# The first block of a weight-stationary unit takes its 256-column matmul first

## The chip, the cores and the metric

The kernel runs on one core of one Trainium2 chip. The metric is the device time of one execution in microseconds. Before the change the median of three runs is 2078.01 us (2077.91 to 2078.08).

## The reference

A two-layer trunk on 256 tokens of width 2048, all in float32. Layer 0 is gated linear attention (4 heads) with an MLP behind it, then one shared K/V projection, then layer 1 with stick-breaking attention (16 query heads on 4 K/V heads) and a second MLP. Every weight is used once. Cut to what matters here:

```python
def sq_relu_mlp(x, w_up, w_down):                  # w_up 2048 x 8192, w_down 8192 x 2048
    return jnp.square(jax.nn.relu(x @ w_up)) @ w_down

h = h + gla_mixer(rms_norm(h, norm1_g[0]), ...)    # q, k, v, r, gate and output projections
h = h + sq_relu_mlp(rms_norm(h, norm2_g[0]), mlp_w_up[0], mlp_w_down[0])
k_sh, v_sh = shared_kv(h, kv_norm_g, kv_w)
h = h + stick_breaking_mixer(rms_norm(h, norm1_g[1]), sb_w_q[0], k_sh, v_sh, sb_w_out[0])
h = h + sq_relu_mlp(rms_norm(h, norm2_g[1]), mlp_w_up[1], mlp_w_down[1])
return rms_norm(h, final_g)
```

## The kernel before, in words

All products keep nearly full float32 precision by splitting: a value is a high part, rounded to the `fp32r` format that TensorE takes, plus a low part, the rest. A product of two split values is three products: high by high, high by low, low by high.

Weights stream from HBM in pieces of 1 MB (128 partitions by 2048 columns, tile `raw`). Each piece is handled as two halves of 1024 columns. For each half ScalarE makes the high part `wh` (L177) and VectorE the low part `wl` = raw - wh (L178). There are three buffers for `wh` and three for `wl`; `next_half()` keeps three halves ready, so that the split of a half starts when TensorE has finished the half three places earlier. `split_weights` shifts each half inside its buffer by a few columns so that all weights of one kind start at the same address modulo 128 columns.

Two kinds of projection use the halves.

- `chunk_n` (through `unit_n` and `half_n`, L232 to L234) keeps activations stationary and streams weights. Each of its matmuls has 512 columns, and three of them (low by high, high by high, high by low) follow each other into one PSUM bank. The second MLP product `dn`, `v`, `r`, `op` and `sv` are of this kind.
- `unit_t` keeps weights stationary and streams activations, so that its result comes out transposed. One unit makes 128 output features for 256 tokens. It goes over 16 blocks `kt` of 128 input features (eight in each half). Its activation tile `act[:, kt, :]` holds the 256 high columns and then the 256 low columns of the block. So a block is two matmuls: `high()` (L199) with `wh` against all 512 columns, and `low()` (L202) with `wl` against the 256 high columns alone. The bank's left half collects wl by high plus wh by high, its right half wh by low; `joined` adds the halves afterwards (ScalarE copy L217, VectorE add L218). Two PSUM banks (`psB`) take turns. The units are `qk` (16), `alow` (1), `up` (128: two MLPs with 4 quarters of 16 units), `sk` (4) and `sq` (16).

`start=True` on a matmul begins a bank's sums anew; all others add. The first block does `high()` and then `low()`, since the full-width matmul begins the sums of the whole bank. The other 15 blocks do `low()` and then `high()`.

An MLP quarter is 16 `up` units followed by four `dn` chunks. In the `qk` and `sq` stages small attention steps are pushed in between the halves (`pump`); their matmuls (`gate`, `cross`, `lev`, `z`, `tail`, `ao`) then stand between those of a unit. The order on each engine is else nearly that of the code; the builder moves a matmul ahead of another whose input is not ready yet at a few places (the first matmul of an MLP stands ahead of some transposes).

Of the kernel before, what the change touches and what calls it, by code (L numbers as in the profile page):

```python
# [16 lines left out]
P = 128  # L17
D = 2048
KT = D // P
T = 256  # L20
# [19 lines left out]
def yoco_kernel(ctx: ExitStack, tc: tile.TileContext, a: dict):  # L40
    nc = tc.nc
    V, S, PE = nc.vector, nc.scalar, nc.tensor
# [36 lines left out]
    def pump(n=1):  # L79
        for _ in range(n):  # L80
            while pending:
                try:
                    next(pending[0])
                    break
                except StopIteration:
                    pending.pop(0)
# [94 lines left out]
    def next_half():  # L181
        while len(ready) < 3:
            n = len(ready)
            prefetch()
            if len(ready) == n:
                break
        return ready.pop(0)


    def unit_t(act, name, steps=1):  # L190
        ps = psB.tile([P, 512], F32, tag="psB", name=name)
        for kt in range(KT):
            if kt % 8 == 0:
                wh, wl = next_half()
            o = (kt % 8) * P
            first, last = kt == 0, kt == KT - 1

            def high():
                PE.matmul(ps, wh[:, o:o + P], act[:, kt, :], start=first, stop=last)  # L199

            def low():
                PE.matmul(ps[:, 0:T], wl[:, o:o + P], act[:, kt, 0:T], start=False, stop=False)  # L202

            if first:
                high()
                low()
            else:
                low()
                high()
            if kt % 8 == 7:  # L210
                pump(steps)
        return ps
# [28 lines left out]
    def chunk_n(act, name):  # L241
        pss = banks(name)
        for kg in range(4):
            unit_n(pss, act, kg)
        return pss
# [278 lines left out]
    def queries_keys():  # L524
        qT = g512("qk", 4, "qT").rearrange("p (f t) -> p f t", f=2)
        kT = g512("qk", 4, "kT").rearrange("p (f t) -> p f t", f=2)
        for dst in (qT, kT):
            for f in range(2):
                joined(unit_t(xg, "qk"), dst[:, f])
        return qT, kT  # L530

    for hd in range(GLA_H):
        st = [half.tile([P, P], F32, tag=f"st{t}", name=f"st{t}", bufs=1) for t in range(NT)]
        sx = half.tile([P, P], F32, tag="sx", name="sx", bufs=1)
        if hd == 0:
            pv, pr = banks("v"), banks("r")
            for kg in range(4):
                unit_n(pv, xg, kg)
                unit_n(pr, xg, kg)
            qT, kT = queries_keys()  # L540
            drain()
            vv = values(pv)
            gs = gates(pr)
            araw = t256("araw")
            spread(rstd0, rbc0, 1.0)
            joined(unit_t(xg, "alow"), araw[0:16], rows=16)
            V.tensor_tensor(alow, araw[0:16], rbc0[0:16], op=ALU.mult)
            give(scores(hd, qT, kT, st, sx))
        else:
            qT, kT = queries_keys()  # L550
            give(scores(hd, qT, kT, st, sx))
            vv = values(chunk_n(xg, "v"))
            gs = gates(chunk_n(xg, "r"))
        give(outputs(hd, st, sx, vv, gs))
# [21 lines left out]
    def mlp(act, rstd2, ssq, after, last=None):  # L576
        for q in range(NQ):
            hT = act_tile("hT", actc if q % 2 else actp)
            for f in range(KT):
                ps = unit_t(act, "up")  # L580
                s = t256("s")
                joined(ps, s)
                y = t256("y")
                V.scalar_tensor_tensor(y, s, 0.0, s, op0=ALU.max, op1=ALU.mult)
                S.copy(hT[:, f, 0:T], y)
                V.tensor_tensor(hT[:, f, T:2 * T], y, hT[:, f, 0:T].bitcast(F32), op=ALU.subtract)
            for c in range(NCH):
                if q == NQ - 1 and c == NCH - 1 and last is not None:
                    last(hT)
                    return  # L590
                ps = chunk_n(hT, "dn")
                for t in range(NT):
                    hc = h[:, t, c * CH:(c + 1) * CH]
                    V.scalar_tensor_tensor(hc, ps[t], rstd2[:, t:t + 1], hc, op0=ALU.mult, op1=ALU.add)
                if q == NQ - 1:
                    squares(ssq, c)
                    after(c)
# [49 lines left out]
    ps = chunk_n(xkv, "sv")  # L647
# [95 lines left out]
    for n in range(KVH):  # L743
        qs = [t512(f"q{t}") for t in range(NT)]
        for g in range(GRP):
            ps = unit_t(xq, "sq", 1 + (len(pending) > 1 or g == GRP - 1))
# [130 lines left out]
```

## Time and profile before

| what | value |
|---|---|
| median of three runs | 2078.01 us |
| the profiled execution's own time | 2078.17 us |
| its span, first to last instruction | 2076.4 us |
| TensorE (PE) busy | 2060.9 us, 99%, 10544 matmuls |
| weight loads (PEld) busy | 1752.9 us, 84% |
| VectorE (DVE) busy | 1311.3 us, 63% |
| ScalarE (ACT) busy | 1038.3 us, 50% |
| DMA engines' mean busy share | 53.7% (queue 1) |
| granted TensorE clock, mean | 0.998 |

TensorE is busy for nearly the whole span, so the time is that of its stream of matmuls. Matmuls overlap in the trace: one is listed with 0.28 us (256 columns) or 0.39 us (512 columns), but the next one starts well before its end. What counts is the distance from the start of one matmul to the start of the next.

### The profile page before, as it was taken

The page shows a single profiled execution, that of the slowest core. Times are in us where ns is not written, and L with a number is a line of the kernel's source. Part 1 is how long each engine was busy: PE and PEld are TensorE (multiplying, and loading weights), DVE is VectorE, ACT ScalarE, POOL GpSimd, SP SyncE. Part 2 cuts the span into 40 slices and gives each one's busy share as a digit, 9 for nine tenths or more (in the row PEclk, how much of TensorE's full clock was granted, in tenths as well). Part 3 has the DMA queues.
Part 4 walks back from the last instruction along what each step waited for, and adds up shares of the span by engine and source line. Part 5 has one row for each costly group of instructions (what it writes and reads, how often), then busy time and mean ns, then how long its engine had stood idle before and what let it go on. Part 6 is the DMA issues. An engine that isn't in the chain of part 4 may idle for free.

```text
span 2076.4 us, 26656 instructions
## 1 busy us (share of the span) xinstructions
PE 2060.9 (99%) x10544; PEld 1752.9 (84%) x10544; DVE 1311.3 (63%) x1804; ACT 1038.3 (50%) x1447; POOL 0.4 (0%) x5
## 2 busy tenths in 40 slices
PE   8999999999999999999999999999999999999998
PEld 7888888888888888888888888888888888888886
DVE  5767776576556556556666687666556556655655
ACT  6645655554344435434555487645345434434543
POOL 0000000000000000000000000000000000000000
PEclk9999999999999999999999999999999999999999
DMA  8544444555555555555555644555555555555553
GB/s 317 183 163 145 160 164 164 183 183 197 189 197 188 200 185 198 189 201 184 201 184 183 208 157 142 183 183 192 193 195 191 197 188 196 190 200 186 198 189 141
DMA packets 55742, 388.40 MB, mean 187 GB/s; under 512 B 6449, under 2 KB 6961, under 8 KB 9153
## 3 DMA queue, kind: packets, MB, share of 16 engines
q1 hardware_dynamic: 55616, 386.70, 53.7%
q8 instruction: 83, 1.36, 0.3%
q14 instruction: 43, 0.34, 0.0%
HBM read 384.58 MB, written 2.10 MB: 186 GB/s over the span
## 4 chain that ended last, share of the span: by engine, by line
PE 99%; DVE 0%; ACT 0%; DMA 0%; issue 0%; DVEq 0%; SPq 0%
PE up L199 22%; PE up L202 11%; PE dn L234 11%; PE dn L233 11%; PE dn L232 11%; PE sq L199 3%; PE op L232 3%; PE op L234 3%; PE op L233 3%; PE qk L199 3%; PE v L232 1%; PE v L234 1%; PE v L233 1%; PE r L232 1%; PE sq L202 1%; PE r L234 1%
## 5 line engine op out<-in xcount | busy, mean ns | idle before, releaser
L178 DVE TENSOR_TENSOR wl<-raw,wh 128x1024 fp32r<-128x1024 f32 (+1 forms) x715 | 874.0, 1223 | 574.9 <-ACT wh L177 562.5
L177 ACT CAST wh<-raw 128x1024 fp32r<-128x1024 f32 (+1 forms) x715 | 750.8, 1051 | 706.1 <-PE dn L233 383.2
L199 PE MATMUL up<-xm,wh 128*128 128x512 f32 x2048 | 693.2, 390 | 0.0
L202 PE MATMUL up<-xm,wl 128*128 128x256 f32 x2048 | 546.3, 277 | 0.0
L199 PEld LDWEIGHTS up<-xm,wh 128*128 128x128 f32 x2048 | 375.4, 188 | 71.5
L202 PEld LDWEIGHTS up<-xm,wl 128*128 128x128 f32 x2048 | 384.4, 188 | 10.7
L234 PE MATMUL dn<-wl,hT 128*128 128x512 f32 x992 | 386.4, 389 | 0.0
L233 PE MATMUL dn<-wh,hT 128*128 128x512 f32 x992 | 386.3, 389 | 0.0
L232 PE MATMUL dn<-wh,hT 128*128 128x512 f32 x992 | 386.0, 389 | 0.0
L233 PEld LDWEIGHTS dn<-wh,hT 128*128 128x128 f32 x992 | 186.2, 188 | 38.8
L234 PEld LDWEIGHTS dn<-wl,hT 128*128 128x128 f32 x992 | 186.2, 188 | 38.5
L232 PEld LDWEIGHTS dn<-wh,hT 128*128 128x128 f32 x992 | 186.2, 188 | 38.4
L217 ACT COPY lo<-up 128x256 f32<-128x256 f32 x128 | 47.7, 373 | 214.2 <-PE up L199 214.2
L218 DVE TENSOR_TENSOR s<-up,lo 128x256 f32<-128x256 f32 x128 | 54.3, 424 | 105.0 <-ACT lo L217 105.0
L233 PE MATMUL op<-wh,oT 128*128 128x512 f32 x256 | 100.5, 393 | 0.0
L232 PE MATMUL op<-wh,oT 128*128 128x512 f32 x256 | 100.5, 393 | 0.0
L234 PE MATMUL op<-wl,oT 128*128 128x512 f32 x256 | 100.0, 391 | 0.0
L199 PE MATMUL sq<-xq,wh 128*128 128x512 f32 x256 | 89.5, 391 | 0.0
L199 PE MATMUL qk<-xg,wh 128*128 128x512 f32 x256 | 88.8, 393 | 0.0
L202 PE MATMUL qk<-xg,wl 128*128 128x256 f32 x256 | 69.3, 281 | 0.0
L202 PE MATMUL sq<-xq,wl 128*128 128x256 f32 x256 | 68.9, 278 | 0.0
L232 PE MATMUL v<-wh,xg 128*128 128x512 f32 x128 | 52.2, 408 | 6.2 <-DVE xg L307 6.2
(207 smaller groups left out, 1836.8 us busy)
## 6 DMA issues: line engine op xcount, KB each, us to landing
raw<-in_w_up SPq DMA_DIRECT2D x128, 1024.0 KB, 4.8
raw<-in_w_down SPq DMA_DIRECT2D x128, 1024.0 KB, 4.8
raw<-in_w_r SPq DMA_DIRECT2D x16, 1024.0 KB, 4.8
raw<-in_w_out SPq DMA_DIRECT2D x16, 1024.0 KB, 4.8
raw<-in_w_sq SPq DMA_DIRECT2D x16, 1024.0 KB, 4.8
raw<-in_w_so SPq DMA_DIRECT2D x16, 1024.0 KB, 4.8
raw<-in_w_v SPq DMA_DIRECT2D x15, 1024.0 KB, 4.9
raw<-in_w_q SPq DMA_DIRECT2D x8, 1024.0 KB, 5.0
```

Of the source, the lines that this page charges most:

```text
L177: S.copy(wh[:, lo:hi], part[:, lo:hi])
L178: V.tensor_tensor(wl[:, lo:hi], part[:, lo:hi], wh[:, lo:hi].bitcast(F32), op=ALU.subtract)
L199: PE.matmul(ps, wh[:, o:o + P], act[:, kt, :], start=first, stop=last)
L202: PE.matmul(ps[:, 0:T], wl[:, o:o + P], act[:, kt, 0:T], start=False, stop=False)
L217: S.copy(lo[0:rows], ps[0:rows, T:2 * T])
L218: V.tensor_tensor(out, ps[0:rows, 0:T], lo[0:rows], op=ALU.add)
L232: PE.matmul(pss[t], xl, wh[:, o:o + CH], start=kt == 0, stop=False)
L233: PE.matmul(pss[t], xh, wh[:, o:o + CH], start=False, stop=False)
L234: PE.matmul(pss[t], xh, wl[:, o:o + CH], start=False, stop=kt == KT - 1)
```

## The change

Only `unit_t` changes. The first block loses its special order: each of the 16 blocks does the 256-column matmul with `wl` and then the 512-column matmul with `wh`. The 256-column matmul of block 0 carries `start=True` for the bank; the 512-column matmul behind it adds to the left half and begins the right half, which nothing has written since the bank was begun. `skip_group_check` only tells the builder not to object to that; it issues nothing.

```diff
             o = (kt % 8) * P
-            first, last = kt == 0, kt == KT - 1
-
-            def high():
-                PE.matmul(ps, wh[:, o:o + P], act[:, kt, :], start=first, stop=last)
-
-            def low():
-                PE.matmul(ps[:, 0:T], wl[:, o:o + P], act[:, kt, 0:T], start=False, stop=False)
-
-            if first:
-                high()
-                low()
-            else:
-                low()
-                high()
+
+            PE.matmul(ps[:, 0:T], wl[:, o:o + P], act[:, kt, 0:T], start=kt == 0, stop=False, skip_group_check=True)
+            PE.matmul(ps, wh[:, o:o + P], act[:, kt, :], start=False, stop=kt == KT - 1, skip_group_check=True)
             if kt % 8 == 7:
                 pump(steps)
```

The count of matmuls, their sizes, and the order on VectorE, ScalarE, GpSimd and the DMA queue stay the same. On TensorE the first two matmuls of each unit trade places. The line numbers of the low and high matmul go from L202 and L199 to L197 and L198; lines behind them move up by 11.

TensorE, inside the second quarter of the first MLP, from the second `up` unit into the third; before:

```order
L202 MATMUL up<-xm,wl 128x256
L199 MATMUL up<-xm,wh 128x512
L199 MATMUL up<-xm,wh 128x512 [waits DVE_49,Activation_49]
L202 MATMUL up<-xm,wl 128x256 [waits DVE_49]
L202 MATMUL up<-xm,wl 128x256
L199 MATMUL up<-xm,wh 128x512
```

and after:

```order
L197 MATMUL up<-xm,wl 128x256
L198 MATMUL up<-xm,wh 128x512
L197 MATMUL up<-xm,wl 128x256 [waits DVE_49]
L198 MATMUL up<-xm,wh 128x512 [waits Activation_49]
L197 MATMUL up<-xm,wl 128x256
L198 MATMUL up<-xm,wh 128x512
```

Before, two 512-column matmuls meet at the boundary and two 256-column ones behind it; after, the two sizes alternate without a break. The wait for VectorE (the low weights, and the bank that `joined` has read) now stands on the first, 256-column matmul, the wait for ScalarE (the high weights) on the second.

TensorE, at the start of the same quarter, where the last `dn` chunk of the quarter before ends and the first `up` unit begins; before:

```order
L233 MATMUL dn_4911<-wh,hT 128x512
L234 MATMUL dn_4911<-wl,hT 128x512
L199 MATMUL up<-xm,wh 128x512 [waits Activation_49]
L202 MATMUL up<-xm,wl 128x256 [waits DVE_49]
L202 MATMUL up<-xm,wl 128x256
L199 MATMUL up<-xm,wh 128x512
```

and after:

```order
L222 MATMUL dn_4911<-wh,hT 128x512
L223 MATMUL dn_4911<-wl,hT 128x512
L197 MATMUL up<-xm,wl 128x256 [waits DVE_49]
L198 MATMUL up<-xm,wh 128x512 [waits Activation_49]
L197 MATMUL up<-xm,wl 128x256
```

Here the alternation now begins with a 256-column matmul right behind a 512-column one of another kind.

TensorE, from the first `up` unit of that quarter into the second; before:

```order
L202 MATMUL up<-xm,wl 128x256
L199 MATMUL up<-xm,wh 128x512
L199 MATMUL up<-xm,wh 128x512 [waits Activation_49]
L202 MATMUL up<-xm,wl 128x256 [waits DVE_49]
L202 MATMUL up<-xm,wl 128x256
```

and after:

```order
L197 MATMUL up<-xm,wl 128x256
L198 MATMUL up<-xm,wh 128x512
L197 MATMUL up<-xm,wl 128x256 [waits DVE_49,PE_49]
L198 MATMUL up<-xm,wh 128x512 [waits Activation_49]
L197 MATMUL up<-xm,wl 128x256
```

The second unit of a quarter gets a wait for TensorE's own count, for a matmul of the quarter before that last wrote this bank.

## Rows read from the trace of the kernel before

**Rows 1.** The page: span, then busy time of each engine.

```profile
span 2076.4 us, 26656 instructions
PE 2060.9 (99%) x10544; PEld 1752.9 (84%) x10544; DVE 1311.3 (63%) x1804; ACT 1038.3 (50%) x1447; POOL 0.4 (0%) x5
```

**Rows 2.** The chain that ended last, shares of the span by engine.

```profile
PE 99%; DVE 0%; ACT 0%; DMA 0%; issue 0%; DVEq 0%; SPq 0%
```

**Rows 3.** Costliest groups, 512-column matmuls of units: count, busy us, mean ns, idle before.

```profile
L199 PE MATMUL up<-xm,wh 128*128 128x512 f32 x2048 | 693.2, 390 | 0.0
...
L199 PE MATMUL sq<-xq,wh 128*128 128x512 f32 x256 | 89.5, 391 | 0.0
L199 PE MATMUL qk<-xg,wh 128*128 128x512 f32 x256 | 88.8, 393 | 0.0
```

**Rows 4.** Waits of PE: total us, times, longest us.

```profile
PE v L232 <- DVE xg L307: 6.2, 1, 6.2
```

**Rows 5.** Timeline of PE, a quarter's start: start us, listed us, instruction.

```profile
588.73 0.39 PE L234 MATMUL dn<-wl,hT 128*128 128x512 f32 x1
...
592.13 0.39 PE L234 MATMUL dn<-wl,hT 128*128 128x512 f32 x1
592.36 0.39 PE L199 MATMUL up<-xm,wh 128*128 128x512 f32 x1
592.59 0.40 PE L202 MATMUL up<-xm,wl 128*128 128x256 f32 x2
592.83 0.39 PE L199 MATMUL up<-xm,wh 128*128 128x512 f32 x1
593.06 0.28 PE L202 MATMUL up<-xm,wl 128*128 128x256 f32 x1
```

**Rows 6.** Timeline of PE, the quarter's first boundary and, last row, its fifteenth.

```profile
597.48 0.28 PE L202 MATMUL up<-xm,wl 128*128 128x256 f32 x1
597.59 0.62 PE L199 MATMUL up<-xm,wh 128*128 128x512 f32 x2
598.05 0.39 PE L202 MATMUL up<-xm,wl 128*128 128x256 f32 x2
598.28 0.40 PE L199 MATMUL up<-xm,wh 128*128 128x512 f32 x1
...
674.22 0.62 PE L199 MATMUL up<-xm,wh 128*128 128x512 f32 x2
```

**Rows 7.** That quarter in one stretch: busy us (count) by engine, clock, DMA, GB/s.

```profile
592.40:679.90 87.50, 87.50 (x513) 77.25 (x512) 57.90 (x79) 43.66 (x62) 0.00 (x0) 1.00 0.56 193
```

**Rows 8.** Timelines of ACT and DVE, the same place (in brackets: idle before).

```profile
592.33 1.05 ACT L177 CAST wh<-raw 128x1024 fp32r<-128x1024 f32 x1 [1.67 <-PE dn L233]
...
593.42 1.23 DVE L178 TENSOR_TENSOR wl<-raw,wh 128x1024 fp32r<-128x1024 f32 x1
...
598.42 0.42 DVE L218 TENSOR_TENSOR s<-up,lo 128x256 f32<-128x256 f32 x1 [0.82 <-ACT lo L217]
```

**Rows 9.** Line L199, the semaphore instructions on the load side: min/median/max ns.

```profile
L199 PEldq EVENT_SEMAPHORE  x125: 51/51/51, 60.5 to 1971.8; - x125
```

**Rows 10.** Timeline of PE, `sq` stage, pairs behind one attention product.

```profile
1201.93 0.40 PE L257 MATMUL z<-lo,both 128*128 128x512 f32 x1
1202.17 0.28 PE L202 MATMUL sq<-xq,wl 128*128 128x256 f32 x1
...
1204.62 0.28 PE L202 MATMUL sq<-xq,wl 128*128 128x256 f32 x1
...
1204.97 0.40 PE L699 MATMUL tail<-hi,upper 128*128 128x512 f32 x1
```

**Rows 11.** Timeline of PE, `sq` stage, pairs behind another such product.

```profile
1227.51 0.40 PE L257 MATMUL z<-lo,both 128*128 128x512 f32 x1
1227.75 0.28 PE L202 MATMUL sq<-xq,wl 128*128 128x256 f32 x1
...
1228.77 0.28 PE L202 MATMUL sq<-xq,wl 128*128 128x256 f32 x1
```

## The prediction

> **What bounds the kernel now.** I read the busy shares first [rows 1]: TensorE 2060.9 of 2076.4 us, VectorE and ScalarE at 63% and 50%. The chain that ended last is 99% TensorE [rows 2], and TensorE's largest wait for another engine is a single 6.2 us at the very start [rows 4]. In one whole `up` quarter TensorE is busy in all 87.50 us, at the full granted clock (1.00, the 2.4 GHz level), while the DMA engines are at 0.56 [rows 7]. So only the distance between matmul starts on TensorE can move the time. I took those from the timeline of PE.
>
> The steady state of a unit is a pair, 256 then 512 columns. From the 256-column matmul at 593.06 to that at 597.48 lie 13 pairs [rows 5, 6]: 4.42 / 13 = 0.340 us a pair. The weights change to another half within these 13 pairs and nothing shows. The `dn` matmuls, 512 columns each, follow each other at (592.13 - 588.73) / 15 = 0.2267 us [rows 5]; that leaves 0.1133 us for 256 columns, just half. Sixteen pairs without any loss would take 16 x 0.340 = 5.440 us.
>
> What a unit really takes stands between the boundaries. A row "x2" of L199 is the last matmul of one unit and the first of the next. From the first such row of the quarter, 597.59, to the fifteenth, 674.22, are 14 units [rows 6]: 76.63 / 14 = 5.474 us. Each unit loses 34 ns (0.0336 us). The pitch is regular up to the boundary, so the loss lies behind it, where two 512-column matmuls meet and then two 256-column ones: 0.46 us from the double row to the next where 2 x 0.2267 = 0.453 is due, and then it trickles out over some four pairs.
>
> **The change part by part.** It adds no matmul and removes none. Three things differ.
>
> First, the break in the alternation at a boundary between two units goes. The numbers of units are the counts of L199 by 16 [rows 3]: 128 `up`, 16 `sq`, 16 `qk`, and five smaller ones. The 128 `up` units stand in 8 quarters of 16, which gives 8 x 15 = 120 boundaries: 120 x 0.0336 = 4.03 us. In the timeline of the other 37 units I count 15 boundaries that run like these (0.50 us) and six where an attention step cuts the loss short after a few matmuls; at half the price that is 0.10 us. The sum is 4.6 us. The bounds of the price: at most all of 0.0336 us, since the pair's 0.340 us is the floor that the trace shows; at least nothing, if the loss belongs to the start of a unit and not to the order (a rival below). I take all of it, because a change of weight half in mid-unit, with waits of its own, costs nothing visible [rows 5, 6].
>
> Second, the start of a stage: the first unit behind a `dn`, `op`, `v`, `r` or `sv` matmul now begins with 256 columns. Before, it begins with 512, and from that start at 592.36 to the unit's last 512-column start at 597.59 are 5.23 us [rows 5, 6], where 15 x 0.2267 + 16 x 0.1133 = 5.213 is due: 17 ns lost. For the new order the trace has no row. If it settles at once, 17 ns are gained; at the price of a boundary another 17 ns are lost. With about 12 such starts that is -0.2 to +0.2 us; I take 0. (That it might not settle at all is the second rival.)
>
> Third, waits. The first matmul of a unit now needs the low weights, which it needed second before, so 0.23 us earlier. The split that ScalarE begins at 592.33, when the last `dn` matmul on its old buffer is through, is done by VectorE at 593.42 + 1.23 = 594.65 [rows 8]. It is two halves ahead of the half begun at 592.36, so it is first used at 597.82 (597.59 + 0.23): 3.2 us of cover. The bank is freed by the add that ends at 598.84 [rows 8] and is needed again one unit later, at about 603.3: 4.4 us. If that cover were gone, what stands behind the waiting matmul on TensorE is all of its stream, so a late split would be paid in full. Six second units of a quarter, and one in `sq`, get a wait on TensorE's own count; in a quarter it is for a matmul before the four `dn` chunks, long done: 0. A matmul that waits for two semaphores brings one more instruction on the load side, 51 ns, 125 times at L199 [rows 9]; most of these go, since the two waits part. I value that at 0: at the boundary shown the matmul waits for one semaphore only, and it loses as much as the later ones that wait for two (the 14 periods hold both kinds, and they are equal).
>
> Nothing is late next: the DMA engines at 0.56 and 193 GB/s [rows 7] would have to deliver 0.6% faster, and the split engines idle between halves.
>
> The sum: the profiled execution took 2078.17 us (span 2076.4, 1.8 around it). 2078.17 - 4.6 = 2073.6, and since it lies 0.16 above the median of the runs, the median after should be 2073.4 us.
>
> **The rivals.**
>
> *The slow cadence (slower).* In the `sq` stage the same alternation, on the same kind of tiles, sometimes runs at another pace: from 1202.17 to 1204.62, 7 pairs, 2.45 / 7 = 0.350 us a pair [rows 10], 10 ns more, steadily, until an attention product ends it. Behind another product it runs at (1228.77 - 1227.75) / 3 = 0.340 [rows 11]. So the alternation has two steady paces, and how it is entered decides. In the `sq` and `qk` stages I count some 77 pairs of the slow kind (0.8 us), nearly all begun by a 256-column matmul right behind a 512-column one of another line; of 14 such beginnings eight were slow. That is just what the change makes at the start of each quarter. And the break that it removes is what put nearly every unit back to the fast pace within four pairs; without it a slow quarter stays slow for 16 x 16 = 256 pairs, 2.56 us. Six quarters start behind `dn`: 6 x 2.56 = 15.4 us, and 2073.4 + 15.4 = 2088.8 us. It loses the gain from two quarters on (4.6 / 2.56 = 1.8), and is slower by 0.2% from four. Against it: the slow beginnings stand behind products that were themselves stretched (0.24 us from 1201.93 to 1202.17 [rows 10]), while `dn` runs at its 0.2267 up to the last [rows 5], and all eight quarters now fall into the fast pace within three matmuls. But the fast one of [rows 11] follows a stretched product too, so that does not settle it. Chance 0.18.
>
> *A few slow quarters.* The same, in one to three quarters, or slow only to the next change of half: 2073.4 + 2.56 to 2073.4 + 7.7, so 2076.0 to 2081.1. Chance 0.12.
>
> *Nothing.* The 34 ns belong to the start of a unit (a new bank, new weights, waits), whatever the order: 2078.0 us. For it: the loss is at every boundary. Against it: the first unit of a quarter, with all of these, loses 17 ns and not 34, and what differs there is the neighbour [rows 5]. The Trainium skill (TensorE: Matmul & The Clock Gate, "Back-to-back issue gap") gives the same outcome by a rule: the gap of a warm matmul is its columns by 2.4 GHz plus 2.5 ns, with no term for its neighbours, so that a new order of the same matmuls changes no sum. By it a pair would take an estimated 325 ns, where the trace has 340; on this trace a unit's time does depend on the order. Chance 0.08.
>
> **How the numbers follow.** The forecast has 0.62: 2073.4, in its own range 2072.5 (the starts gain 0.2 and the 0.8 us of slow pairs in `sq` and `qk` go too) to 2074.3 (the same with the other sign). 0.2% is 4.16 us, about what a measurement here can tell from no change; faster by that means below 2073.85, which is 0.54 of the 0.62. Within 0.2%: the other 0.08, the few slow quarters 0.12 and nothing 0.08, together 0.28. Slower: 0.18. The range for 8 in 10 goes from 2072.5 to 2081.5 and leaves out the slow cadence in most quarters.
>
> **What would show it.** Right: in the `up` quarters no row of L197 or L198 is double, and from the last matmul of the first unit to that of the fifteenth are 14 x 5.440 = 76.16 us instead of 76.63; TensorE's busy time falls by about 4.6 us, and the semaphore instructions at the unit's lines fall from 125 to a handful. Wrong: pairs at 0.350 us through whole quarters (the slow cadence); a period that is still 5.474 (nothing); a wait of PE for `wl` or `s` in the list of waits (the cover was not there).

## The result, and the profile after

The changed kernel takes 2093.49 us, the median of four executions (2090.83 to 2094.87), against 2078.05 for the kernel before on the same chip: a ratio of 1.0071, with a 95% interval of 1.0059 to 1.0083. It is slower by 15 us. The forecast was 2073.4 us, and the time lies outside its range of 2072.5 to 2081.5; the rival called the slow cadence is what happened. One execution of e3 below ran at a granted clock of 0.589 and took 3287.44 us; it is left out of e3's ratio, and every other execution in this document ran at 0.998 or 0.999.

The page of the profiled execution (2090.83 us), span and busy time, answers to [rows 1]:

```profile
span 2089.0 us, 26538 instructions
...
PE 2072.8 (99%) x10544; PEld 1760.3 (84%) x10544; DVE 1312.3 (63%) x1804; ACT 1039.2 (50%) x1447; POOL 0.4 (0%) x5
```

The span grew by 12.6 us and TensorE's busy time by 11.9, with the same 10544 matmuls. 118 instructions are gone: nearly all the semaphore instructions of [rows 9]. The wait that follows is TensorE's largest for another engine (total, times, longest); it stands at the start of the kernel, as in [rows 4]. No wait of an `up` matmul for `wl` or `s` is in the list:

```profile
PE v L221 <- ACT wh L177: 6.7, 2, 5.6
```

The costliest group of matmuls answers to [rows 3]:

```profile
L198 PE MATMUL up<-xm,wh 128*128 128x512 f32 x2048 | 712.3, 394 | 0.0
```

A 512-column `up` matmul is listed with 394 ns instead of 390, and nothing stands idle before it. It is the matmuls themselves that go slower. The timeline of PE shows how, at the start of the first quarter, then over the second quarter and to the third (start us, listed us):

```profile
417.76 0.28 PE L197 MATMUL up<-xm,wl 128*128 128x256 f32 x1
...
592.67 0.40 PE L223 MATMUL dn<-wl,hT 128*128 128x512 f32 x1
592.90 0.28 PE L197 MATMUL up<-xm,wl 128*128 128x256 f32 x1
...
682.15 0.28 PE L197 MATMUL up<-xm,wl 128*128 128x256 f32 x1
...
769.56 0.28 PE L197 MATMUL up<-xm,wl 128*128 128x256 f32 x1
```

From 592.90 to 682.15 are 255 pairs: 89.25 / 255 = 0.350 us a pair, from the first pair to the last, where [rows 5, 6] have 0.340. No row of `up` is double there: the loss at the boundaries is gone, and 10 ns a pair have come in its place. One quarter pays 255 x 0.010 = 2.55 us and gets back 15 x 0.0336 = 0.50. All six quarters that begin behind `dn` are like this one. The first and the fifth, which begin among transposes, ran at 0.340 in this execution. The windows view sets the second quarter beside the first (columns as in [rows 7]):

```profile
592.90:682.10 89.20, 89.20 (x511) 78.12 (x510) 57.82 (x79) 43.78 (x62) 0.00 (x0) 1.00 0.55 189
419.30:505.70 86.40, 86.40 (x511) 76.46 (x510) 59.10 (x88) 45.10 (x71) 0.00 (x0) 1.00 0.55 193
```

The same 511 matmuls take 89.20 us in one and 86.40 in the other; TensorE is busy all of the time in both, the granted clock is 1.00 (the 2.4 GHz level) in both, and the DMA share is 0.55 in both. Neither a wait nor the clock nor the transfers make the difference.

The sum: six quarters at 2.55 and 120 boundaries at 0.0336 make 15.3 - 4.0 = 11.3 us; the profiled executions differ by 2090.83 - 2078.17 = 12.7. Of the remaining 1.4 us, 1.0 lies ahead of the first `up` (417.76 against 416.74), and that part differs from one execution to the next (e7 below). Most of the rest is in `sq`, which has slow stretches too. Its first five units stand behind an `sv` matmul, also of 512 columns, and run at 27.65 / 79 = 0.350 us a pair, in the timeline of PE:

```profile
1171.06 0.28 PE L197 MATMUL sq<-xq,wl 128*128 128x256 f32 x1
...
1198.71 0.28 PE L197 MATMUL sq<-xq,wl 128*128 128x256 f32 x1
```

In all of `sq` 146 pairs go at 0.350 us, where the kernel before has 56: 0.9 us more, against which stands what its boundaries give back.

The other stages that use the same unit need not be slow. The start of `qk`, behind an `r` matmul of 512 columns, in the timeline of PE:

```profile
53.98 0.28 PE L197 MATMUL qk<-xg,wl 128*128 128x256 f32 x1
...
75.40 0.28 PE L197 MATMUL qk<-xg,wl 128*128 128x256 f32 x1
```

The code and the order are those of `up`, and 63 pairs take 21.42 us: 0.340 each. So the new order does not by itself mean the slow pace. One thing that is not the same is where the tiles lie: `split_weights` puts the weights of `qk` at `XG_AT` = 56 and those of `up` and `sq` at `X_AT` = 32, and the activations lie at matching places. The places of `qk` do not exclude the slow pace, though: behind a `cross` matmul ten pairs of `qk` go at 0.350 (169.09 to 172.59), as at this spot in the kernel before.

### The profile page after: what moved, and what is told of

It is laid out like the page before. It is cut to its first block, busy times and chain, and to the rows that moved or that the text cites. A ratio compares the mean times of both kernels' runs of the same rounds, so it can differ in the third digit from the quotient of the medians.

```text
span 2089.0 us, 26538 instructions
## 1 busy us (share of the span) xinstructions
PE 2072.8 (99%) x10544; PEld 1760.3 (84%) x10544; DVE 1312.3 (63%) x1804; ACT 1039.2 (50%) x1447; POOL 0.4 (0%) x5
## 4 chain that ended last, share of the span: by engine, by line
PE 99%; DVE 0%; ACT 0%; DMA 0%; SPq 0%; issue 0%; DVEq 0%
PE up L198 23%; PE up L197 11%; PE dn L223 11%; PE dn L221 11%; PE dn L222 11%; PE sq L198 3%; PE op L221 3%; PE op L223 3%; PE op L222 3%; PE qk L198 3%; PE v L221 1%; PE sq L197 1%; PE r L221 1%; PE v L222 1%; PE v L223 1%; PE r L223 1%
## 5 line engine op out<-in xcount | busy, mean ns | idle before, releaser
L198 PE MATMUL up<-xm,wh 128*128 128x512 f32 x2048 | 712.3, 394 | 0.0
L197 PE MATMUL up<-xm,wl 128*128 128x256 f32 x2048 | 572.5, 280 | 0.0
L198 PEld LDWEIGHTS up<-xm,wh 128*128 128x128 f32 x2048 | 384.9, 188 | 86.9
L197 PEld LDWEIGHTS up<-xm,wl 128*128 128x128 f32 x2048 | 384.5, 188 | 0.3
L198 PE MATMUL sq<-xq,wh 128*128 128x512 f32 x256 | 90.3, 393 | 0.0
L198 PE MATMUL qk<-xg,wh 128*128 128x512 f32 x256 | 88.6, 391 | 0.0
L197 PE MATMUL qk<-xg,wl 128*128 128x256 f32 x256 | 72.0, 281 | 0.0
L197 PE MATMUL sq<-xq,wl 128*128 128x256 f32 x256 | 71.4, 279 | 0.0
```

What stands on the lines that cost most here:

```text
L198: PE.matmul(ps, wh[:, o:o + P], act[:, kt, :], start=False, stop=kt == KT - 1, skip_group_check=True)
```

## The experiments

The theory: the alternation has two steady paces; how a stage is entered decides which; a stage entered slowly stays slow since no break resets it; and the tiles' addresses decide the entry. The rivals: the beginning of the sums with a 256-column matmul costs time in every unit; the slow pace belongs to `up`'s addresses whatever the entry; the old order would gain from other addresses as much.

**e1: the first unit of each quarter in the old order, all else as changed.**

```diff
-    def unit_t(act, name, steps=1):
+    def unit_t(act, name, steps=1, high_first=False):
...
+            if kt == 0 and high_first:
+                PE.matmul(ps, wh[:, o:o + P], act[:, kt, :], start=True, stop=False)
+                PE.matmul(ps[:, 0:T], wl[:, o:o + P], act[:, kt, 0:T], start=False, stop=False)
+            else:
...
-                ps = unit_t(act, "up")
+                ps = unit_t(act, "up", 1, f == 0)
```

> The changed kernel, but the first unit of each MLP quarter keeps the old order of its first block (512 columns first); all other units stay in the new order. Theory 'the entry decides' (the pace of the alternation is set where it begins behind a dn matmul, and a boundary between two units neither changes nor breaks it): all eight up quarters run at 0.340 us a pair, a unit in 5.440 us, and the time falls by the six slow quarters, 15.3 us, to 2073 to 2075 us. Rival 'the alternation drifts' (a long unbroken alternation falls into 0.350 by itself or at a unit boundary): most quarters turn slow after some units, 2080 to 2091 us.

2074.24 us (2074.06 to 2074.94), ratio 0.9981 [0.9972, 0.9990]. In the timeline of PE, the start of the second quarter and its last pair:

```profile
591.04 0.39 PE L198 MATMUL up<-xm,wh 128*128 128x512 f32 x1
...
591.74 0.28 PE L201 MATMUL up<-xm,wl 128*128 128x256 f32 x1
...
677.76 0.28 PE L201 MATMUL up<-xm,wl 128*128 128x256 f32 x1
```

253 pairs in 86.02 us: 0.340. Two matmuls that trade places once in 512, eight times in the kernel, take away 19 us. The other 120 `up` units still begin their sums with 256 columns, at the same addresses, and run at the fast pace, all eight quarters alike: the first two rivals fall, and so does a drift into the slow pace. `sq`, where e1 changes nothing, is the check: behind `sv` its 79 pairs still go at 0.350 (1162.05 to 1189.70).

**e2: the reverse, only the first unit of each quarter in the new order.** As e1, with `f > 0` for `up` and the old order in `qk`, `alow`, `sk` and `sq`.

```diff
-                ps = unit_t(act, "up", 1, f == 0)
+                ps = unit_t(act, "up", 1, f > 0)
...
-            ps = unit_t(xq, "sq", 1 + (len(pending) > 1 or g == GRP - 1))
+            ps = unit_t(xq, "sq", 1 + (len(pending) > 1 or g == GRP - 1), True)
```

> The reverse: only the first unit of each MLP quarter takes the new order, every other unit keeps the old one. Theory 'the entry decides, and the old break resets': six first units run their 15 or 16 pairs at 0.350 (6 x 0.15 us), the next boundary puts the pace back, so 2078.5 to 2079.5 us. Rival 'the break does not reset': the quarters stay slow behind a slow first unit, 2090 us or more.

2079.40 us (2078.72 to 2081.95), ratio 1.0006 [0.9997, 1.0016]. The timeline of PE, the first and the second unit of the second quarter (L201 and L202 are pairs; L198 and L199 are the block in the old order that begins a unit):

```profile
595.06 0.28 PE L201 MATMUL up<-xm,wl 128*128 128x256 f32 x1
...
600.31 0.28 PE L201 MATMUL up<-xm,wl 128*128 128x256 f32 x1
...
601.69 0.28 PE L201 MATMUL up<-xm,wl 128*128 128x256 f32 x1
...
605.77 0.28 PE L201 MATMUL up<-xm,wl 128*128 128x256 f32 x1
```

The first unit goes at (600.31 - 595.06) / 15 = 0.350, the second at (605.77 - 601.69) / 12 = 0.340. The entry makes the pace, and the break that cost 34 ns puts it right. In the first quarter it took two breaks; the first of them and the pairs behind it:

```profile
425.74 0.40 PE L198 MATMUL up<-xm,wh 128*128 128x512 f32 x1
...
426.10 0.28 PE L201 MATMUL up<-xm,wl 128*128 128x256 f32 x1
...
431.00 0.28 PE L201 MATMUL up<-xm,wl 128*128 128x256 f32 x1
```

The 14 pairs behind that break still go at 4.90 / 14 = 0.350, and only the next boundary ends it. The fifth quarter entered fast, and the other six are like the second. So six breaks of seven restored the fast pace. By the trace the quarters lose 1.0 us together (six times 0.12 and once 0.25). The median rose by 1.3 us, as expected for this theory, but the interval alone does not tell it from no change; against the rival's 2090 us it is clear.

**e3: the changed order, with the weights and activations of `up` and `sq` at the places that `qk` uses.**

```diff
-    X_AT, XG_AT, KV_AT = 32, 56, 120
+    X_AT, XG_AT, KV_AT = 56, 56, 120
...
-    xm = x_tile("xm", 0)
+    xm = x_tile("xm", 24)
...
-            holder["q"] = x_tile("xq", 0)
+            holder["q"] = x_tile("xq", 24)
...
-    xm2 = x_tile("xm2", 0)
+    xm2 = x_tile("xm2", 24)
```

> The changed kernel with the unit tiles of the MLPs and of sq at the places of qk, whose units entered the fast pace: activations 24 columns in, weights at 56 (wl) and 40 (wh) instead of 32 and 16. Order and sizes are untouched. Theory 'the entry is an address matter' (the load of wl meets the last 512-column matmul's stream in the memory, as its start 0.237 instead of 0.227 us later shows): all six quarters enter fast, 2072 to 2075 us. Rival 'the order alone' (behind dn the alternation is slow wherever the tiles lie): 2089 to 2095 us.

2072.59 us (six of seven executions: 2071.90 to 2073.06), ratio 0.9972 [0.9961, 0.9984]. The timeline of PE, the second quarter and the start of the third:

```profile
591.06 0.39 PE L223 MATMUL dn<-wl,hT 128*128 128x512 f32 x1
591.28 0.28 PE L197 MATMUL up<-xm,wl 128*128 128x256 f32 x1
...
677.99 0.28 PE L197 MATMUL up<-xm,wl 128*128 128x256 f32 x1
...
765.36 0.28 PE L197 MATMUL up<-xm,wl 128*128 128x256 f32 x1
```

255 pairs in 86.71 us: 0.340, in all eight quarters. A quarter with its `dn` chunks takes 765.36 - 591.28 = 174.08 us, where the changed kernel needs 769.56 - 592.90 = 176.66. Instructions and order are the same; only the places moved, 24 columns further, those of the weights and of the activations together. That is the whole loss and more. In `sq`, which moved as well, the slow pairs fall from 146 to one.

**e4: `dn` and the other streamed weights at 96 instead of 120, `up` as changed.**

```diff
-            to = 120 if at is None else at - (16 if k == 0 else 0)
+            to = 96 if at is None else at - (16 if k == 0 else 0)
```

> The changed kernel with the streamed weights of all chunks (dn, v, r, op, sv) at 96 instead of 120, so that up's wl lies to them as qk's wl did. Theory 'the entry is an address matter': the up quarters enter at 0.227 and run fast, 2072 to 2075 us, if the chunks themselves keep 0.2267 us a matmul; if they do not, every 1 ns on their 4,617 matmuls costs 4.6 us on top, and the entry is read from the trace. Rival 'the order alone': the entry stays at 0.237 and the quarters at 0.350, 2089 us or more.

2115.57 us (2115.42 to 2117.00), ratio 1.0181 [1.0165, 1.0198]. The timeline of PE, the end of `dn` and the second quarter, then the third quarter:

```profile
595.67 0.40 PE L223 MATMUL dn<-wl,hT 128*128 128x512 f32 x1
...
600.59 0.40 PE L223 MATMUL dn<-wl,hT 128*128 128x512 f32 x1
600.82 0.28 PE L197 MATMUL up<-xm,wl 128*128 128x256 f32 x1
...
690.07 0.28 PE L197 MATMUL up<-xm,wl 128*128 128x256 f32 x1
...
780.39 0.28 PE L197 MATMUL up<-xm,wl 128*128 128x256 f32 x1
...
867.11 0.28 PE L197 MATMUL up<-xm,wl 128*128 128x256 f32 x1
```

The `dn` matmuls go at 4.92 / 21 = 0.2343 us instead of 0.2267 [rows 5]: over the 3 x 992 of them 22.6 us, and more in the other chunks. The second quarter is slow (89.25 / 255 = 0.350), the third fast (86.72 / 255 = 0.340); so are the other even and odd ones. As a test of the entry it is inconclusive, since it moved the pace of `dn` as well. What alternates from quarter to quarter in the code is the buffer of `hT` (`actp` or `actc`), which the last `dn` matmul reads; that fits, but no run isolated it. The run does show that the chunks' pace depends on addresses too.

**e5: the old order at e3's addresses.** The edit is e3's, on the kernel before.

```diff
-    X_AT, XG_AT, KV_AT = 32, 56, 120
+    X_AT, XG_AT, KV_AT = 56, 56, 120
...
```

> The kernel before (old order of the first block) with the addresses of the run before last: activations of the MLPs and of sq 24 columns in, their weights at 56 and 40. Theory 'order and entry add up' (the order is worth 34 ns a boundary wherever the entry is fast; the addresses only choose the entry): the units still take about 5.474 us, so 2077 to 2078.5 us, and the new order on the same addresses is 4.5 to 5 us faster. Rival 'the addresses alone are the gain' (at these places the old break costs nothing either): 2073 us, as the new order had there.

2077.29 us (2076.97 to 2077.97), ratio 0.9994 [0.9984, 1.0004]. Its first and fifteenth boundary in the timeline of PE:

```profile
598.46 0.62 PE L199 MATMUL up<-xm,wh 128*128 128x512 f32 x2
...
675.09 0.62 PE L199 MATMUL up<-xm,wh 128*128 128x512 f32 x2
```

76.63 / 14 = 5.474 us a unit, exactly that of [rows 6]: the old order keeps its boundary loss and gains little from the addresses. The third rival falls. Between e5 and e3 only the order differs: (0.9994 - 0.9972) x 2078 = 4.6 us, the gain that the forecast's first step gave. Each ratio is known to about 0.001, or 2 us, so that the exact agreement is luck; the rows give (5.474 - 16 x 0.340) x 120 = 4.1 us for the `up` boundaries.

**e6: `wh` at the place of `wl`.**

```diff
-            to = 120 if at is None else at - (16 if k == 0 else 0)
+            to = 120 if at is None else at - (0 if k == 0 else 0)
```

> The changed kernel with wh of the unit weights at the same place as wl (32 for up) and not 16 columns before it; nothing else. Theory 'the paces come from where the weight load and the stream read at the same time': the pace of a pair is something else than 0.340 or 0.350 us, for qk too, which entered fast. Rival 'the two paces are a matter of instruction timing alone': 0.340 and 0.350 stay, 2090 to 2095 us.

2091.91 us, one execution. The timeline of PE, 63 pairs of `qk`, 14 of `up` in the second quarter and 242 in the fifth:

```profile
52.53 0.28 PE L197 MATMUL qk<-xg,wl 128*128 128x256 f32 x1
...
74.79 0.28 PE L197 MATMUL qk<-xg,wl 128*128 128x256 f32 x1
...
594.95 0.28 PE L197 MATMUL up<-xm,wl 128*128 128x256 f32 x1
...
599.81 0.28 PE L197 MATMUL up<-xm,wl 128*128 128x256 f32 x1
...
1380.73 0.28 PE L197 MATMUL up<-xm,wl 128*128 128x256 f32 x1
...
1466.23 0.28 PE L197 MATMUL up<-xm,wl 128*128 128x256 f32 x1
```

`qk` goes at 22.26 / 63 = 0.353. `up` goes at 4.86 / 14 = 0.347 in seven quarters and at 85.50 / 242 = 0.353 in the fifth. There are more than two paces, and moving `wh` by 16 columns was enough to change that of a stage that was fast. The two values 0.340 and 0.350 are a property of the placement, not of the alternation as such; that one stage can run at either of two values is found at this placement too.

**e7: the changed kernel once more.** No edit.

> The changed kernel once more, for a second profile, since its runs spread over 4 us. Theory 'the entry decides': the six quarters behind dn are slow again in full (255 pairs at 0.350), and what differs between executions is the pace of places where the entry hangs on a wait: the two quarters behind transposes, and sk and sq. Rival 'the pace wanders': slow and fast stretches change inside quarters.

2094.82 us, one execution. The timeline of PE, the first quarter:

```profile
416.37 0.28 PE L197 MATMUL up<-xm,wl 128*128 128x256 f32 x1
...
418.38 0.28 PE L197 MATMUL up<-xm,wl 128*128 128x256 f32 x1
...
506.23 0.28 PE L197 MATMUL up<-xm,wl 128*128 128x256 f32 x1
```

251 pairs in 87.85 us: 0.350, in the very quarter that ran at 0.340 in the first profile. All eight are slow here. Two more slow quarters are 5.1 us and the first `up` starts 1.4 us earlier (416.37 against 417.76): 3.7 us together, and the two executions differ by 4.0. That is as much as the spread of the changed kernel's four times (2090.83 to 2094.87); the others have no profile.

**e8: one break in mid-quarter.** As e1, with the old order in the ninth unit instead of the first.

```diff
-                ps = unit_t(act, "up", 1, f == 0)
+                ps = unit_t(act, "up", 1, f == 8)
```

> The changed kernel with the old order of the first block in one unit of each quarter, the ninth, so that the alternation is broken once in mid-quarter. Theory 'the pace is a memory of the entry': the first eight units of a quarter that enters slow run at 0.350, the last eight at 0.340 us a pair; per slow quarter 8 x 16 x 10 ns = 1.28 us come back, 7.7 us over six quarters and 10.2 over eight, so 2083 to 2085 us. Rival 'something of the quarter holds the slow pace' (its tiles, its neighbours on the other engines): the ninth unit is disturbed and the tenth is slow again, 2090 to 2095 us.

2086.56 us (2083.88 to 2087.28), ratio 1.0037 [1.0024, 1.0051]. The timeline of PE, the second quarter before and behind its break, then the fifth from its break on:

```profile
590.88 0.28 PE L201 MATMUL up<-xm,wl 128*128 128x256 f32 x1
...
635.33 0.28 PE L201 MATMUL up<-xm,wl 128*128 128x256 f32 x1
635.68 0.39 PE L198 MATMUL up<-xm,wh 128*128 128x512 f32 x1
...
636.37 0.28 PE L201 MATMUL up<-xm,wl 128*128 128x256 f32 x1
...
678.53 0.28 PE L201 MATMUL up<-xm,wl 128*128 128x256 f32 x1
...
1414.91 0.40 PE L198 MATMUL up<-xm,wh 128*128 128x512 f32 x1
...
1415.62 0.28 PE L201 MATMUL up<-xm,wl 128*128 128x256 f32 x1
...
1459.02 0.28 PE L201 MATMUL up<-xm,wl 128*128 128x256 f32 x1
```

In the second quarter 127 pairs take 44.45 us (0.350) ahead of the break and 124 take 42.16 (0.340) behind it. Six of the seven slow quarters do this. In the fifth the 124 pairs behind the break still take 43.40 us (0.350): there the break did not reset. The first quarter was fast throughout. So a break mostly restores the fast pace, and not always: with e2, 12 of the 14 breaks that met the slow pace did. At those 12 the break's first 512-column matmul is listed with 0.39 us, at the other two with 0.40, and these two lie in quarters that begin among transposes. The profiled execution is the fastest of the four; the median lies above the 2083 to 2085 us that were expected, and what the other three did is not known.

**e9: e3 once more, with more executions.** The edit is e3's.

> The new order with the addresses of qk once more, in more rounds, as the version that beats both: 2072 to 2073 us, 0.25 to 0.3% under the kernel before. If the two quarters behind transposes can enter slow here as well, single executions at 2075 or 2078 us.

2072.06 us (2071.72 to 2074.23), ratio 0.9971 [0.9961, 0.9982], the fastest version. Its page, to be read beside [rows 1] and the changed kernel's:

```profile
PE 2054.3 (99%) x10544; PEld 1749.7 (85%) x10544; DVE 1311.7 (63%) x1804; ACT 1038.1 (50%) x1447; POOL 0.4 (0%) x5
...
L198 PE MATMUL up<-xm,wh 128*128 128x512 f32 x2048 | 696.9, 389 | 0.0
```

The line to look at is that of `up`: 389 ns, where the changed kernel has 394. At these places all eight quarters enter fast (of `sq`, five pairs are slow), and the change brings what it was forecast to bring. TensorE's busy time is 6.6 us below that of the kernel before; by e5 about 1 us of the gain belongs to the places and the rest to the order.

## Why the prediction was wrong

**The bound** was right: the distance between matmul starts alone moved the time, and no engine or transfer became late.

**The first step, the boundaries, 4.6 us,** was right in mechanism and size. The double rows and the 34 ns are gone; e5 against e3 measures 4.6 us, give or take some 3.

**The second step, the start of a stage, "I take 0", is the one that failed.** It allowed -0.2 to +0.2 us and left a start that does not settle to a rival. Measured: 2.55 us in each of six to eight starts of an `up` quarter, 15 to 20 us, and 0.8 us at the start of `sq` behind `sv`. The step had looked at the 17 ns of the entry alone. What an entry costs is the 10 ns a pair times the length of the stretch that inherits it, and the change made that stretch 16 times longer by taking the breaks out of it.

**The reason given against the rival** failed too. `dn` holds its 0.2267 us to the last [rows 5], but in that trace the last `dn` matmul runs beside the load of `up`'s high weights. The change puts the load of the low weights there. The weight loads of `up` in the timelines of PEld, before (beside the `dn` matmul of 592.13 [rows 5]) and after (beside that of 592.67):

```profile
592.14 0.19 PEld L199 LDWEIGHTS up<-xm,wh 128*128 128x128 f32 x1
...
592.67 0.19 PEld L197 LDWEIGHTS up<-xm,wl 128*128 128x128 f32 x1
```

That matmul is now listed at 0.40 us instead of 0.39, and the pairs behind it go at 0.350. In e3, with the tiles elsewhere, it is listed at 0.39 again and the pairs go at 0.340. And "all eight quarters now fall into the fast pace within three matmuls" was true because of the order that the change removes: e1 puts it back in eight places and has the fast pace again. Whether the stretched `dn` matmul causes the slow pace or is its first sign is not shown: [rows 11] has a fast entry behind a stretched product.

**The third step, the waits, 0,** was right: no `up` matmul waits for `wl` or `s`, and the 118 instructions less brought no gain that shows beside that of the boundaries.

**The rival's price,** 2088.8 us, took six quarters, those behind `dn`; the execution with six slow quarters took 2090.83. It left out `sq` behind `sv`. e7 shows that the two quarters behind transposes can be slow as well: 2088.8 + 2 x 2.55 = 2093.9, where e7 took 2094.82. Its chance of 0.18 was too low: the trace of before had eight slow ones among 14 beginnings of this kind, more than half. All of them lie in `sq`, whose tiles lie at `up`'s places; that made them better evidence for `up` than the prediction took them for. The only slow stretch of `qk` in that trace, ten pairs, begins with a 512-column matmul behind a `cross` matmul of 128 columns.

**The rival "nothing" with its rule.** The same matmuls in another order cost 15 us here, and one trade of places a quarter (e1) gives them back. The Trainium skill (TensorE: Matmul & The Clock Gate, "Back-to-back issue gap") gives the rule with columns and clock alone as the gap of an isolated matmul, and says that in a stream of loads and matmuls both set the spacing. So the page does not promise that the order is free, as the prediction read it; in these runs it is not.

**What stays open.** Shown: the pace of one and the same stream depends on where its tiles lie in SBUF (e3, e4, e6), it is taken on at entry (e1, e2), and a break usually resets it (e2, e8). Not shown: what meets what, and which tile's place matters, since e3 moved weights and activations together. A conflict between a weight load and the reading of the moving columns would fit, but no run isolated it. The Trainium skill (SBUF — State Buffer, "Who interferes with whom") lists two read ports of TensorE as independent, with contention only on the pair that VectorE and GpSimd share. With 0.4 us of work on GpSimd that rule gives no reason for a pace that depends on addresses, and these runs show such a pace; they do not say which part of the path is to blame. Open too are why the first quarter differed between two executions of one program, and why one break of e2 and one of e8 failed.

## What to carry to other kernels

A break in a regular pattern that costs a few nanoseconds may also be what ends a slow stretch: before removing it, look in the trace for stretches of the same pattern at another pace, and price the entry over the whole stretch that will inherit it. Count such stretches where the operands lie as in the stage that will change, before giving a chance. Where matmuls of equal shape and clock go at different paces, move a tile by a few columns before changing the order; here 24 columns and the new order together made 2072.1 us out of 2078.

## What the runs showed of the hardware

At a granted clock of 1.00, TensorE being busy throughout, a pair of 256 and 512 columns took 0.340, 0.347, 0.350 or 0.353 us, and a 512-column matmul 0.2267 or 0.2343 us, depending on the places of the tiles and, at the changed kernel's places and at e6's, on the entry as well. Over the whole kernel that makes 43.5 us: e4 and e9 run the same matmuls in the same order and take 2115.57 and 2072.06 us, on two chips on which the kernel before took 2078.08 and 2078.27. The pace has a memory: an entry that differs by one trade of two matmuls was still to be seen 255 pairs and 89 us later.
